# A fused attention, recurrence and convolution layer: first scales in the first input block, one matmul less at the start, last store from ACT, SBUF slots held back from the gates

## The chip, the cores and the metric

The kernel runs on one core of a Trainium2 chip. The metric is the device time of one execution in microseconds. A core has a matmul engine (PE), a vector engine (DVE), an activation engine (ACT), a general engine (POOL) and an engine that only issues transfers (SP). They run side by side, each in the order of its own instruction stream, and wait for one another by semaphores. Matmul results land in PSUM, which has 8 banks; everything else lies in SBUF.

## The reference

The kernel computes one layer of a sequence model for 512 positions and 1024 channels. Everything is float32.

```python
h = rmsnorm(x, norm_mix_g)
z = h @ w_in          # fq fk fv ff | hq hf hi hg | ca cb | gl   (gl: 3 gates of 1024)
ya = fox_attention(rmsnorm(fq), rmsnorm(fk), fv, log_sigmoid(ff))   # 6 heads of 64
yb = hgrn2_chunkwise(hq, -expm1(logf), hi, logf)                    # 4 heads, state 128 x 96
yb = rmsnorm(yb) * silu(hg)
yc = silu(layernorm(causal_dwconv(ca * sigmoid(cb))))               # 256 channels, 31 taps
gates = sigmoid(gl + gate_b)
x = x + (gates[0]*(ya @ wb_a) + gates[1]*(yb @ wb_b) + gates[2]*(yc @ wb_c)) @ w_out
h2 = rmsnorm(x, norm_ffn_g)
gate_in, value_in = split(h2 @ w_up)
x = x + (silu(causal_dwconv(gate_in)) * value_in) @ w_down
```

## The kernel before

Activations lie transposed: 8 blocks `x0` to `x7` of 128 channels by 512 positions. Every block is scaled with its column of `g1` (the first norm's gain) and split by `split_scaled` into a high and a low part, `x0h` and `x0l`. ACT makes the high part and DVE the low part. The weights come in units of 128 x 1024 (`wr_`, the raw load), which ACT copies to a high part (`wh_`) and DVE subtracts to a low part (`wl_`). A product is three matmuls, high x high, low x high and high x low, so that one weight unit takes 24 matmuls of 512 columns.

**The order is made before the program runs.** `body` does not issue instructions; it records them in program order with a `Plan`. `Plan.schedule` then plays the whole list through with assumed durations, engine by engine. Whenever an engine is free it takes the ready instruction with the lowest priority number, which is the program position plus a base such as `FIRST` or `EVAC`. The result is a fixed instruction stream for every engine. An instruction may only be taken if all tiles that it opens fit: `CAPS` gives the number of slots of each kind. The main ones are 75 SBUF slots `s` of 128 x 512, 8 PSUM banks `ps`, and at most 5 of these banks for the long products (`mm`) and 6 for everything else (`aux`). A DVE instruction that opens no new slot is never held back by this rule.

The stages, in program order: the product for `hi` (PSUM tiles `him`), whose first matmul needs `x0h` and the first weights `wr_hi`; `cb` and `ca`, the input of the convolution (`xca`); four HGRN heads, each with `hf` and `hq` products, transposes `khT`, chunk states `pst` and `st`, seven levels (for each a DVE difference `d`, two ACT exponentials, a DVE product `ql`, PE matmuls `pl`, and for the five short levels a masked copy `COPY_PREDICATED` of the result into `at`), then `pi`; the fox projections between the heads; six fox heads, each with scores `sp`, a DVE instruction that adds the mask `cB` to the scores and takes the minimum (`dd`, and the read of its accumulator `mn`), an exponential `pp`, transposes `ptp` and the result `po`; `conv()` with 60 taps, each one DVE instruction `cv<-xca,pr,cv`, 30 for each of two blocks; the `hg` products and their evacuation `xhg`; then the gates.

A gate is a unit `gl` of 24 matmuls; there are 24 of them (`gl00`, `gl01`, `gl02`, `gl10`, ...), recorded behind the heads and the convolution, so that in the stream they serve as filling between the heads' short matmuls. `evac` moves a gate from its PSUM bank to an SBUF slot, `gr`, with one DVE instruction, and frees the bank. The slot then stays taken until the branch products (`br`) use it. After that come `wo`, the feed-forward products `ug` and `uv`, and `dn`; each of the last 8 outputs is added to the residual on DVE and stored.

The lines of `schedule` that decide whether an instruction may be taken:

```python
need = {}
for n in op.uses:
    if n not in live:
        for k in self.kind[n]:
            need[k] = need.get(k, 0) + 1
if all(used[k] + c <= self.caps[k] for k, c in need.items()):
```

In the profile all instructions recorded through the plan stand on line L110, so that groups are told apart by the names of their tiles.

Of the kernel before, what the change touches and what calls it, by code (L numbers as in the profile page):

```python
# [10 lines left out]
F32 = mybir.dt.float32  # L11
# [36 lines left out]
for _name, _w in (("ident", 128), ("ones", 128), ("onesD", 32)):  # L48
# [1 line left out]
    _n += _w  # L50
NCST = _n
CAPS = {"s": 75, "bm": 2, "tiny": 24, "wraw": 3, "whi": 3, "wlo": 3, "ps": 8, "mm": 5, "aux": 6,
        "d": 2, "ed": 3, "cB": 4, "dd": 3, "pp": 3, "pT": 8}
NCB = NM * (NM + 1) // 2 * P
NLV = 2
NAHEAD = 6
NWARM = 5
FIRST, WPREP, STAT, EVAC, YOUT = -4000000, -3000000, -2000000, -1000000, -1000000


# [4 lines left out]
class Plan:  # L65
# [73 lines left out]
    def schedule(self):  # L139
        ops = self.ops  # L140
        last = {}
        for op in ops:
            op.left = len(op.deps)
            op.ready = 0.0
            for d in op.deps:
                d.users.append(op)
            for n in op.uses:
                last[n] = last.get(n, 0) + 1
        used = {k: 0 for k in self.caps}
        live = set()  # L150
        free = {e: 0.0 for e in ("tensor", "vector", "scalar", "gpsimd", "sync")}
        soon = {e: [] for e in free}
        now_ = {e: [] for e in free}
        releases = []
        for op in ops:
            if not op.left:
                heapq.heappush(soon[op.eng], (op.ready, op.seq, op))
        t, done, order = 0.0, 0, []
        while done < len(ops):
            while releases and releases[0][0] <= t:  # L160
                _, n = heapq.heappop(releases)
                for k in self.kind[n]:
                    used[k] -= 1
            for e in free:
                while soon[e] and soon[e][0][0] <= t:
                    op = heapq.heappop(soon[e])[2]
                    heapq.heappush(now_[e], (op.pri, op.seq, op))
            moved = False
            for e in free:
                if free[e] > t or not now_[e]:  # L170
                    continue
                put = []
                while now_[e]:
                    it = heapq.heappop(now_[e])
                    op = it[2]
                    need = {}
                    for n in op.uses:
                        if n not in live:
                            for k in self.kind[n]:
                                need[k] = need.get(k, 0) + 1  # L180
                    if all(used[k] + c <= self.caps[k] for k, c in need.items()):
                        for n in op.uses:
                            live.add(n)
                            last[n] -= 1
                        for k, c in need.items():
                            used[k] += c
                        op.start = t
                        op.end = t + op.dur
                        free[e] = op.end
                        for n in op.uses:  # L190
                            if not last[n]:
                                heapq.heappush(releases, (op.end + op.lat, n))
                        for u in op.users:
                            hop = 0.0 if (u.eng == e == "tensor") else op.lat
                            u.ready = max(u.ready, op.end + hop)
                            u.left -= 1
                            if not u.left:
                                heapq.heappush(soon[u.eng], (u.ready, u.seq, u))
                        order.append(op)
                        done += 1  # L200
                        moved = True
                        break
                    put.append(it)
                for it in put:
                    heapq.heappush(now_[e], it)
            if moved:
                continue
            nxt = [f for e, f in free.items() if f > t and now_[e]]
            nxt += [s[0][0] for s in soon.values() if s and s[0][0] > t]
            nxt += [max(s[0][0], free[e]) for e, s in soon.items() if s]  # L210
            if releases:
                nxt.append(releases[0][0])
            nxt = [x for x in nxt if x > t]
            if not nxt:
                raise RuntimeError("no instruction can start: " + str(
                    {e: [(o[2].seq, o[2].uses) for o in now_[e][:3]] for e in now_}) + str(used))
            t = min(nxt)
        self.length = max(op.end for op in ops)
        return order
# [57 lines left out]


@with_exitstack
def body(ctx: ExitStack, tc, xT, wct, wt3, wt1, wdn, par, cst, rst, msk, cmk, out):  # L280
    cpool = ctx.enter_context(tc.tile_pool(name="cpool", bufs=1))
    spool = ctx.enter_context(tc.tile_pool(name="spool", bufs=CAPS["s"]))
    wpool = ctx.enter_context(tc.tile_pool(name="wpool", bufs=3))
# [8 lines left out]
    def nm(name):  # L292
        cnt[0] += 1
        return f"{name}_{cnt[0]}"

    def slot(name, dt=F32, kind=None):
        return nc.tile(spool, [P, S], dt, "s", nm(name), ("s", kind) if kind else ("s",))
# [14 lines left out]
    def pc(name, i=0, n=1):  # L312
        o, _ = PCOLS[name]
        return pr[:, o + i:o + i + n]
# [57 lines left out]
    def split_scaled(src, g, name):  # L372
        hi = slot(name + "h", F32R)
        nc.scalar.activation(hi, src, AF.Copy, scale=g)
        lo = slot(name + "l", F32R)
        nc.vector.scalar_tensor_tensor(lo, src, g, hi.bitcast(F32), op0=ALU.mult, op1=ALU.subtract)
        return hi, lo

    def evac(ps, name, rb):
        with nc.at(EVAC):  # L380
            t = slot(name)
            nc.vector.tensor_tensor(t, ps, rb, op=ALU.mult)
        return t

# [62 lines left out]
    with nc.at(FIRST):  # L447
        nc.table("sigmoid_and_others")
        for _ in range(NWARM):
            nc.tensor.matmul(wps[:, :256], warm[:, :P], warm[:, :256], start=True, stop=True)  # L450
    cuts = ((0, 1), (1, 2), (2, 3), (3, 4), (4, 6), (6, 8))
    xg, w0, sums = [], [], []
    xs = [slot(f"x{kt}") for kt in range(KT)]

    def first_weights():
        k0, k1 = cuts[len(w0)]
        src = wt3[k0 // 2][:, (k0 % 2) * 384:(k0 % 2) * 384 + (k1 - k0) * 384]
        raw = nc.tile(bpool, [P, 2 * S], F32, "bm", nm("wr_hi"), ("bm",)) if len(w0) in (3, 4) else None
        w0.append(wunit(src, (k1 - k0) * 384, f"hi{len(w0)}", FIRST, raw))

    for kt in range(KT):
        with nc.at(FIRST):
            nc.sync.dma_start(xs[kt], xT[:, kt, :])
            if kt == 0:
                nc.sync.dma_start(pr[:, :KT], par[:, :KT])
            if kt == 4:
                nc.sync.dma_start(pr[:, KT:], par[:, KT:])
        if kt in (0, 1, 2, 3, 5):
            first_weights()
        with nc.at(FIRST):  # L470
            xg.append(split_scaled(xs[kt], pc("g1", kt), f"x{kt}"))
        with nc.at(STAT):
            q = slot(f"n1sq{kt}")
            added = nc.scalar.activation(q, xs[kt], AF.Square)
            if kt:
                nc.vector.tensor_tensor(sums[0], sums[0], q, op=ALU.add)
            else:
                sums.append(q)
# [448 lines left out]
    merged, gates, x1, xg2 = [], [], [], []  # L927

    def gate(n):
        gates.append([evac(gemm_c(15 + 3 * n + br, xg, f"gl{n}{br}"), f"gr{n}{br}", rb1) for br in range(3)])  # L930

    def merge(n):
        gts = gates[n]
# [59 lines left out]
    for n in range(KT):  # L993
        parts = ((0, S),) if n < KT - 1 else ((0, S // 2), (S // 2, S))
        ps = bank(f"dn{n}", "mm")
        ws = [wunit(wdn[n][:, k0 * P:min(NF, k0 + 8) * P], (min(NF, k0 + 8) - k0) * P, f"wd{n}{k0}")
              for k0 in range(0, NF, 8)]
        for w, k0 in zip(ws, range(0, NF, 8)):
            gemm_unit(ps, w, gT[k0:k0 + 8], k0 == 0, k0 + 8 >= NF)
        for c0, c1 in parts:  # L1000
            with nc.at(EVAC):
                nc.vector.tensor_tensor(x1[n][:, c0:c1], ps[:, c0:c1], x1[n][:, c0:c1], op=ALU.add)
            nc.sync.dma_start(out[n][:, c0:c1], x1[n][:, c0:c1])

    nc.issue(tc)

# [1 line left out]
def _layout(i):  # L1008
# [49 lines left out]
    for L in LEVELS:  # L1058
# [4 lines left out]
    c = np.ascontiguousarray  # L1063
    return {
        "xT": c(x.T.reshape(KT, P, S).transpose(1, 0, 2)), "wct": c(wct), "wt3": c(wt3), "wt1": c(wt1),
        "wdn": c(wdn), "par": c(par), "cst": c(cst), "rst": c(rst), "msk": c(msk), "cmk": c(cmk)}


_ORDER = ("xT", "wct", "wt3", "wt1", "wdn", "par", "cst", "rst", "msk", "cmk")


# [14 lines left out]
```

## Time and profile before

| | before |
|---|---|
| time, median of 3 runs (lowest, highest) | 804.49 us (804.33, 804.51) |
| the profiled execution's own time | 804.38 us |
| its span in the trace | 802.5 us |
| PE busy | 797.6 us, 99% of the span |
| DVE busy | 496.4 us, 62% |
| ACT busy | 336.6 us, 42% |
| POOL busy | 86.0 us, 11% |
| mean granted clock of PE | 0.999 of full speed |

The span is the stretch from the first to the last event of the trace; the profiled execution's time is 1.9 us longer. The busy share is an average over the stages.

### The profile page before, as it was taken

The numbers are of one execution on the slowest core, as the hardware profiler recorded it, in microseconds if no ns is written. First come the engines' busy times: TensorE is split into PE (matmuls) and PEld (weight loads), VectorE is DVE, ScalarE is ACT, GpSimd is POOL, SyncE is SP. The second block draws the span as 40 slices with busy tenths as digits, with TensorE's granted clock in tenths as the row PEclk, the third lists the DMA queues.
The fourth block names the chain that finished last, engine by engine and source line by source line (L and its number), as shares of the span: only waits on it lengthen the run. The fifth ranks groups of instructions, "written<-read, shape, count | busy, mean of one in ns | idle before, by whom it ended". The sixth has DMA issues, their size and how long they took to land.

```text
span 802.5 us, 10175 instructions
## 1 busy us (share of the span) xinstructions
PE 797.6 (99%) x3911; PEld 677.0 (84%) x3911; DVE 496.4 (62%) x804; ACT 336.6 (42%) x547; POOL 86.0 (11%) x78
## 2 busy tenths in 40 slices
PE   9999999999999999999999999999999999999998
PEld 8889999888888888888888888888888888888886
DVE  6588898988888878556655465555555455222221
ACT  7247556554656328433244254333333333111110
POOL 2000000100122000114422021111101111000000
PEclk9999999999999999999999999999999999999999
DMA  8522132422477222323422322322322332334320
GB/s 306 182 69 83 60 118 79 106 100 79 120 166 181 93 104 80 118 103 133 145 97 87 119 84 100 105 94 91 105 100 85 105 99 82 102 112 128 101 86 26
DMA packets 30880, 86.96 MB, mean 108 GB/s; under 512 B 3640, under 2 KB 7786, under 8 KB 30832
## 3 DMA queue, kind: packets, MB, share of 16 engines
q1 hardware_dynamic: 28240, 82.39, 30.3%
q0 software_dynamic: 2592, 3.93, 3.2%
q8 instruction: 30, 0.49, 0.3%
q14 instruction: 18, 0.15, 0.1%
HBM read 84.17 MB, written 2.14 MB: 108 GB/s over the span
## 4 chain that ended last, share of the span: by engine, by line
PE 99%; DVE 0%; DVEq 0%; issue 0%
PE gl L110 17%; PE ug L110 15%; PE uv L110 15%; PE dn L110 15%; PE br L110 5%; PE wo L110 5%; PE hf L110 3%; PE hq L110 3%; PE pl L110 3%; PE fvm L110 2%; PE him L110 2%; PE f0m L110 2%; PE f1m L110 2%; PE hg L110 2%; PE cb L110 1%; PE ca L110 1%
## 5 line engine op out<-in xcount | busy, mean ns | idle before, releaser
L110 DVE TENSOR_TENSOR wl_wd<-wr_wd,wh_wd 128x1024 fp32r<-128x1024 f32 (+1 forms) x24 | 27.3, 1136 | 65.9 <-ACT wh_wd L110 65.9
L110 ACT CAST wh_wd<-wr_wd 128x1024 fp32r<-128x1024 f32 (+1 forms) x24 | 23.6, 983 | 85.6 <-PE dn L110 81.8
L110 DVE TENSOR_TENSOR wl_ug<-wr_ug,wh_ug 128x1024 fp32r<-128x1024 f32 x22 | 27.0, 1225 | 49.6 <-ACT wh_ug L110 49.6
L110 POOL TENSOR_TENSOR fy<-fy,n2rB 128x512 f32<-128x512 f32 x22 | 28.9, 1317 | 207.8 <-ACT fy L110 207.8
L110 DVE SCALAR_TENSOR_TENSOR cv<-xca,pr,cv 128x511 f32<-128x511 f32 (+29 forms) x60 | 43.5, 729 | 0.3
L110 ACT CAST wh_uv<-wr_uv 128x1024 fp32r<-128x1024 f32 x22 | 23.2, 1054 | 44.4 <-PE ug L110 37.0
L110 ACT CAST wh_gl<-wr_gl 128x1024 fp32r<-128x1024 f32 x24 | 25.3, 1053 | 35.2 <-PE gl L110 21.4
L110 POOL DMA_DIRECT2D cB<-cdr x18 | 16.0, 1093 | 213.7 <-DMA cdr<-cT 122.8
L110 ACT CAST wh_ug<-wr_ug 128x1024 fp32r<-128x1024 f32 x22 | 23.2, 1055 | 31.1 <-PE uv L110 23.6
L110 POOL TENSOR_TENSOR gr<-gr,gr 128x512 f32<-128x512 f32 x14 | 21.6, 1546 | 113.9 <-DVE gr L110 113.2
L110 DVE SCALAR_TENSOR_TENSOR fy<-ug,pr,fy 128x511 f32<-128x511 f32 (+1 forms) x44 | 32.8, 747 | 1.0 <-ACT fy L110 0.3
L110 DVE TENSOR_TENSOR wl_gl<-wr_gl,wh_gl 128x1024 fp32r<-128x1024 f32 x24 | 31.5, 1311 | 2.3 <-ACT wh_gl L110 2.2
L110 DVE TENSOR_TENSOR gr<-gl,n1rB 128x512 f32<-128x512 f32 x24 | 16.6, 692 | 25.3 <-PE gl L110 25.3
L110 DVE TENSOR_TENSOR wl_uv<-wr_uv,wh_uv 128x1024 fp32r<-128x1024 f32 x22 | 27.0, 1225 | 8.5 <-ACT wh_uv L110 8.5
L110 DVE TENSOR_TENSOR ug<-ug,n2rB 128x512 f32<-128x512 f32 x22 | 15.1, 691 | 25.4 <-PE ug L110 25.3
L110 ACT ACTIVATE fy<-fy 128x512 f32<-128x512 f32 x22 | 13.9, 632 | 39.4 <-DVE fy L110 39.4
L110 PEld LDWEIGHTS pl<-ql,kl 128*128 128x128 f32 (+2 forms) x224 | 21.3, 161 | 2.2 <-issue 0.8
L110 DVE TENSOR_TENSOR x<-dn,x 128x512 f32<-128x512 f32 (+1 forms) x9 | 5.6, 631 | 27.3 <-PE dn L110 27.3
L110 PE MATMUL pl<-ql,kl 128*128 128x64 f32 (+2 forms) x224 | 21.3, 242 | 0.0
L110 DVE TENSOR_TENSOR gr<-gr,br 128x512 f32<-128x512 f32 x24 | 16.2, 682 | 5.5 <-PE br L110 5.4
L110 ACT ACTIVATE fy<-ug,pr 128x512 f32<-128x512 f32 x22 | 17.8, 812 | 1.9 <-DVE ug L110 1.9
L110 DVE TENSOR_TENSOR d<-bm 128x520 f32<-128x520 f32 (+5 forms) x24 | 18.1, 773 | 0.0
(1128 smaller groups left out, 2540.2 us busy)
## 6 DMA issues: line engine op xcount, KB each, us to landing
wr_gl<-wct SPq DMA_DIRECT2D x24, 512.0 KB, 3.2
wr_ug<-wct SPq DMA_DIRECT2D x22, 512.0 KB, 3.3
wr_uv<-wct SPq DMA_DIRECT2D x22, 512.0 KB, 3.3
wr_wd<-wdn SPq DMA_DIRECT2D x16, 512.0 KB, 3.5
x<-xT SPq DMA_DIRECT2D x16, 256.0 KB, 4.6
wr_wb<-wct SPq DMA_DIRECT2D x8, 512.0 KB, 3.2
wr_wo<-wct SPq DMA_DIRECT2D x8, 512.0 KB, 3.1
wr_wd<-wdn SPq DMA_DIRECT2D x8, 384.0 KB, 3.1
```

The lines of the kernel that those rows point to most:

```text
L110: op.fn = lambda: fn(*args, **kw)
```

## The change

It has four parts.

1. A new input `x0g` of 128 x 520 holds the first block of `x` and, behind it, the 8 columns of `g1`. One transfer brings both into a tile of the `bm` pool; the separate transfer of `pr[:, :8]` goes. DVE copies the 8 columns to `pr` for the later blocks; the first block's two scalings read them from the new tile. The raw tile of the fifth `hi` weight load moves from the `bm` pool to the `wraw` pool.
2. The warm-up at the start, 5 matmuls of 256 columns on zeros, becomes 4 of 256 and 1 of 128.
3. The last output block is stored in two halves; the second half's store is issued from ACT's queue instead of SP's.
4. The gates' slots get a kind of their own, `gr` (up to 24, as many as there are), and `schedule` takes an instruction that opens such a slot only if 3 more `s` slots would stay free behind it.

```diff
-        "d": 2, "ed": 3, "cB": 4, "dd": 3, "pp": 3, "pT": 8}
+        "d": 2, "ed": 3, "cB": 4, "gr": 24, "dd": 3, "pp": 3, "pT": 8}
-NWARM = 5
+NWARM = 4
@@ Plan.schedule
-                    if all(used[k] + c <= self.caps[k] for k, c in need.items()):
+
+                    spare = 3 if "gr" in need else 0
+                    if all(used[k] + c + (spare if k == "s" else 0) <= self.caps[k] for k, c in need.items()):
@@ body
-    def evac(ps, name, rb):
+    def evac(ps, name, rb, kind=None):
         with nc.at(EVAC):
-            t = slot(name)
+            t = slot(name, kind=kind)
             nc.vector.tensor_tensor(t, ps, rb, op=ALU.mult)
         return t
...
             nc.tensor.matmul(wps[:, :256], warm[:, :P], warm[:, :256], start=True, stop=True)
+        nc.tensor.matmul(wps[:, :P], warm[:, :P], warm[:, :P], start=True, stop=True)
-    xs = [slot(f"x{kt}") for kt in range(KT)]
+
+    x0 = nc.tile(bpool, [P, 2 * S], F32, "bm", nm("x0"), ("bm",))
+    xs = [x0[:, :S]] + [slot(f"x{kt}") for kt in range(1, KT)]
...
-        raw = nc.tile(bpool, [P, 2 * S], F32, "bm", nm("wr_hi"), ("bm",)) if len(w0) in (3, 4) else None
+        raw = nc.tile(bpool, [P, 2 * S], F32, "bm", nm("wr_hi"), ("bm",)) if len(w0) == 3 else None
...
-            nc.sync.dma_start(xs[kt], xT[:, kt, :])
             if kt == 0:
-                nc.sync.dma_start(pr[:, :KT], par[:, :KT])
+                nc.sync.dma_start(x0[:, :S + KT], x0g)
+                nc.vector.tensor_copy(pr[:, :KT], x0[:, S:S + KT])
+            else:
+                nc.sync.dma_start(xs[kt], xT[:, kt, :])
...
-            xg.append(split_scaled(xs[kt], pc("g1", kt), f"x{kt}"))
+            xg.append(split_scaled(xs[kt], pc("g1", kt) if kt else x0[:, S:S + 1], f"x{kt}"))
...
-        gates.append([evac(gemm_c(15 + 3 * n + br, xg, f"gl{n}{br}"), f"gr{n}{br}", rb1) for br in range(3)])
+        gates.append([evac(gemm_c(15 + 3 * n + br, xg, f"gl{n}{br}"), f"gr{n}{br}", rb1, "gr") for br in range(3)])
...
-            nc.sync.dma_start(out[n][:, c0:c1], x1[n][:, c0:c1])
+            (nc.sync if c1 - c0 == S or c0 == 0 else nc.scalar).dma_start(out[n][:, c0:c1], x1[n][:, c0:c1])
```

Since the order of every stream is made by `schedule`, the fourth part moves instructions on all engines from the first gate on. Three places follow, with the program's names and numbers of tiles (the second number of a name is only a serial number).

DVE's stream before, at the last `hg` evacuation (`xhg2`) and the mask-add of the first fox head's first scores (`dd_434`):

```order
L110 TENSOR_SCALAR nlk_380_467<-u_376_463,l1m_188 128x512
L110 ISA dd_434_521,mn_436_523<-sp_435_522,cB_427_514 128x128
L110 ISA mn_436_523 128x1
L110 TENSOR_TENSOR xhg2_689_776<-hg2_688_775,n1rB_78_158 128x512
L110 TENSOR_TENSOR bm_379_466<-bm_379_466,nlk_380_467 128x512
```

DVE's stream of the change from the same place on. `xhg2` stands 37 instructions before `dd_434`, and between the first and the last lines shown here stand 30 taps in all (5 of `cv0`, 25 of `cv1`, the last 20 of them in one row), three `wl_gl`, `qe` and `pr0`:

```order
L110 TENSOR_SCALAR nlk_380_467<-u_376_463,l1m_188 128x512
L110 TENSOR_TENSOR xhg2_689_776<-hg2_688_775,n1rB_78_158 128x512
L110 TENSOR_TENSOR bm_379_466<-bm_379_466,nlk_380_467 128x512
L110 TENSOR_TENSOR wl_gl02_711_798<-wr_gl02_709_796,wh_gl02_710_797 128x1024
...
L110 TENSOR_TENSOR wl_gl11_721_808<-wr_gl11_719_806,wh_gl11_720_807 128x1024
L110 SCALAR_TENSOR_TENSOR cv1_650_737<-xca1_102_182,pr_80,cv1_650_737 128x501
...
L110 SCALAR_TENSOR_TENSOR cv1_650_737<-xca1_102_182,pr_80,cv1_650_737 128x483
L110 SCALAR_TENSOR_TENSOR cv1_650_737<-xca1_102_182,pr_80,cv1_650_737 128x482
L110 ISA dd_434_521,mn_436_523<-sp_435_522,cB_427_514 128x128
L110 ISA mn_436_523 128x1
```

So `dd_434` moved from just before `xhg2` to 37 instructions behind it. The first gate's evacuation `gr00` stands 38 instructions behind `dd_434` in the change.

PE's stream before, at the transposes `khT_337` of HGRN head 2, which take the PSUM bank of `sp_435` and so wait for DVE's read of it:

```order
L110 MATMUL hg2_688_775<-x7h_47_127,wl_hg2_687_774 128x512
L110 MATMUL gl00_702_789<-x0h_14_94,wh_gl00_700_787 128x512
L110 MATMUL gl00_702_789<-x0l_15_95,wh_gl00_700_787 128x512
L110 MATMUL gl00_702_789<-x0h_14_94,wl_gl00_701_788 128x512
L110 MATMUL khT_337_424<-cs_78,kh_336_423 128x128 x3
L110 MATMUL gl00_702_789<-x1h_20_100,wh_gl00_700_787 128x512
```

PE's stream of the change at the same transposes:

```order
L110 MATMUL gl01_707_794<-x7l_48_128,wh_gl01_705_792 128x512
L110 MATMUL gl01_707_794<-x7h_47_127,wl_gl01_706_793 128x512
L110 MATMUL khT_337_424<-cs_78,kh_336_423 128x128 x3
L110 MATMUL pl_343_430<-ql_58_138,kl0_54_134 65x64 x4
L110 MATMUL pl_346_433<-ql_58_138,kl1_55_135 33x32 x8
L110 MATMUL pa_362_449<-pr0_361_448,cs_78 128x4
L110 MATMUL pl_349_436<-ql_58_138,kl0_54_134 128x64 x4
```

Before, three matmuls of the gate `gl00` stand between the last `hg` matmul and `khT_337`, and the rest of the gates fills in behind it. In the change all 48 matmuls of `gl00` and `gl01` stand ahead of it, and behind it no gate matmul follows until `gl02`, after 9 levels of `pl` (of heads 2 and 3), a second `khT`, six `pst`, seven `pi`, two `pa`, six `ptp` and four `sp`.

ACT's stream at the start, before:

```order
L137 ACT_TABLE_LOAD
L110 ACTIVATE n1sq0_16_96<-x0_3_83 128x512
L110 ACTIVATE x0h_14_94<-x0_3_83,pr_80 128x512
L110 CAST wh_hi0_12_92<-wr_hi0_11_91 128x384
L110 ACTIVATE x1h_20_100<-x1_4_84,pr_80 128x512
```

and in the change:

```order
L137 ACT_TABLE_LOAD
L110 ACTIVATE x0h_14_94<-x0_3_83 128x512
L110 CAST wh_hi0_12_92<-wr_hi0_11_91 128x384
L110 ACTIVATE n1sq0_16_96<-x0_3_83 128x512
L110 ACTIVATE x1h_20_100<-x1_4_84,pr_80 128x512
```

The square `n1sq0` moved behind the two instructions for which the first matmul waits.

## Rows read from the trace of the kernel before

**Rows 1.** The page: span, busy time of each engine, shares of the chain.

```profile
span 802.5 us, 10175 instructions
PE 797.6 (99%) x3911; PEld 677.0 (84%) x3911; DVE 496.4 (62%) x804; ACT 336.6 (42%) x547; POOL 86.0 (11%) x78
PE 99%; DVE 0%; DVEq 0%; issue 0%
```

**Rows 2.** Waits of PE: total us, times, longest us.

```profile
PE warm L110 <- DVE warm L110: 1.2, 1, 1.2
```

**Rows 3.** The chain of waits at head 2: start us, us, what.

```profile
162.27 16.35 PE hg L110 x72
...
179.31 0.33 PE khT L110 x3
...
186.14 0.64 PE pl L110 x16
...
188.59 0.84 PE pl L110 x8
...
191.10 0.84 PE pl L110 x8
```

**Rows 4.** The timeline of DVE at the end of `hg`: start us, us, instruction.

```profile
177.74 0.28 DVE L110 CUSTOM_DVE_ANT_0 dd<-sp,cB 128x128 f32<-128x128 f32 x1
...
178.66 0.69 DVE L110 TENSOR_TENSOR xhg<-hg,n1rB 128x512 f32<-128x512 f32 x1 [0.63 <-PE hg L110]
```

**Rows 5.** The timeline of DVE where four taps run in a row.

```profile
286.99 2.99 DVE L110 SCALAR_TENSOR_TENSOR cv<-xca,pr,cv 128x486 f32<-128x486 f32 x4
```

**Rows 6.** Groups of DVE by tile: count, busy us, mean ns, idle before.

```profile
L110 DVE SCALAR_TENSOR_TENSOR cv<-xca,pr,cv 128x511 f32<-128x511 f32 (+29 forms) x60 | 43.5, 729 | 0.3
L110 DVE TENSOR_TENSOR wl_gl<-wr_gl,wh_gl 128x1024 fp32r<-128x1024 f32 x24 | 31.5, 1311 | 2.3 <-ACT wh_gl L110 2.2
L110 DVE TENSOR_TENSOR d<-bm 128x520 f32<-128x520 f32 (+5 forms) x24 | 18.1, 773 | 0.0
L110 DVE CUSTOM_DVE_ANT_0 dd<-sp,cB 128x128 f32<-128x128 f32 (+3 forms) x24 | 11.2, 482 | 2.6 <-PE sp L110 1.4 <-DMA cB<-cdr 1.2
L110 DVE COPY_PREDICATED at<-mk,pl 128x256 f32<-128x256 uint8 x20 | 11.2, 560 | 3.9 <-PE pl L110 3.2 <-ACT kl L110 0.3
L110 DVE TENSOR_TENSOR ql<-ed,xq 128x256 f32<-128x256 f32 x24 | 10.0, 421 | 1.4 <-ACT ed L110 0.8 <-PE pl L110 0.6
```

**Rows 7.** Windows: length, busy PE PEld DVE ACT POOL, PEclk, DMA share, GB/s.

```profile
5.70:20.00 14.30, 14.27 (x80) 13.56 (x79) 12.60 (x21) 12.74 (x21) 0.66 (x2) 1.00 0.98 356
179.00:235.00 56.00, 56.00 (x380) 49.12 (x379) 47.79 (x115) 32.60 (x84) 6.60 (x8) 1.00 0.43 112
235.00:273.00 38.00, 38.00 (x223) 32.67 (x222) 32.47 (x84) 21.16 (x47) 5.72 (x7) 1.00 0.61 152
801.00:802.50 1.50, 0.00 (x0) 0.00 (x0) 0.00 (x0) 0.00 (x0) 0.00 (x0) 0.50 0.05 17
```

**Rows 8.** The timeline of the start.

```profile
1.18 0.42 SPq L110 DMA_DIRECT2D pr<-par  x1
1.19 4.63 PE L110 MATMUL warm<-warm 128*128 128x256 f32 x10 [1.19 <-DVE warm L110]
3.62 0.63 ACT L110 ACTIVATE n1sq<-x 128x512 f32<-128x512 f32 x1 [1.60 <-DMA x<-xT]
4.89 0.75 DVE L110 SCALAR_TENSOR_TENSOR x0l<-x,pr,x0h 128x512 fp32r<-128x512 f32 x1 [3.76 <-ACT x0h L110]
5.31 1.02 PE L110 MATMUL him<-wh_hi,x0h 128*128 128x384 f32 x3
```

**Rows 9.** The timeline of the end.

```profile
798.46 0.39 PE L110 MATMUL dn<-gT21h,wl_wd 128*128 128x512 f32 x1
798.89 0.76 DVE L110 TENSOR_TENSOR x<-dn,x 128x256 f32<-128x256 f32 x2 [13.36 <-PE dn L110]
799.34 0.82 SPq L110 DMA_DIRECT2D out<-x  x2
```

More of the change, by code (lines that the diff above doesn't have):

```diff
@@ L279, in body @@
 @with_exitstack
-def body(ctx: ExitStack, tc, xT, wct, wt3, wt1, wdn, par, cst, rst, msk, cmk, out):
+def body(ctx: ExitStack, tc, xT, wct, wt3, wt1, wdn, par, cst, rst, msk, cmk, x0g, out):
     cpool = ctx.enter_context(tc.tile_pool(name="cpool", bufs=1))
@@ L1065, in _layout @@
         "xT": c(x.T.reshape(KT, P, S).transpose(1, 0, 2)), "wct": c(wct), "wt3": c(wt3), "wt1": c(wt1),
-        "wdn": c(wdn), "par": c(par), "cst": c(cst), "rst": c(rst), "msk": c(msk), "cmk": c(cmk)}
-_ORDER = ("xT", "wct", "wt3", "wt1", "wdn", "par", "cst", "rst", "msk", "cmk")
+        "wdn": c(wdn), "par": c(par), "cst": c(cst), "rst": c(rst), "msk": c(msk), "cmk": c(cmk),
+        "x0g": c(np.concatenate([x.T[:P], par[:, :KT]], 1))}
+_ORDER = ("xT", "wct", "wt3", "wt1", "wdn", "par", "cst", "rst", "msk", "cmk", "x0g")
 def kernel(**inputs):
```

## Prediction

> **What bounds the kernel now.** I read the page first. PE is busy for 99% of the span, and the chain that ended last runs through PE alone [rows 1]. The waits of PE say the same: it waited once, 1.2 us for the memset of the warm-up [rows 2]. So no pause of PE is left to remove behind the start, and whatever makes PE stand adds to the time in full. Next I read who could make it stand. DVE is busy 62% on average, but in the stretch of the HGRN and fox heads it is 47.79 of 56 us and then 32.47 of 38, both 85%, while PE runs without a gap [rows 7]. There DVE's order decides when PE's short matmuls may start, and the gate matmuls that stand between them give it the time. A change of order in that stretch is the first thing to look at; the start and the end are small beside it.
>
> **Part 4, the slots held back, term A: the transposes of head 2.** In the order of before, DVE's mask-add `dd_434` stands just ahead of `xhg2`, and in the trace it began at 177.74, before `xhg2` at 178.66 [rows 4]. PE's `khT_337`, which waits for it, came at 179.31 without a wait [rows 3]. In the new order `dd_434` stands 37 instructions behind `xhg2`. `xhg2` cannot start before the last `hg` matmul, which is the same place in both orders. From there DVE has to do, before PE may begin `khT_337`:
> - 20 taps in a row. Four in a row took 2.99 us [rows 5], so 0.747 each, 14.9 in all.
> - 10 more taps at the mean of 0.729 [rows 6], 7.3.
> - three `wl_gl` at 1.31 [rows 6], 3.9.
> - `xhg2` at 0.69 [rows 4], `bm` and `qe`, of the same 512 columns, at the same; `pr0` about 0.15; `dd_434` with its read 0.3 [rows 4]. Together 2.5.
>
> That is 28.6 us. In the meantime PE has the 48 matmuls of `gl00` and `gl01`. The 72 `hg` matmuls of the same form took 16.35 [rows 3], so 0.227 each, 10.9 in all. DVE starts some 0.2 after PE does, because it reads what PE's last `hg` matmul wrote. PE then stands 28.6 + 0.2 - 10.9 = 17.9 us. The bounds are 16.9 (the three `wl_gl` and all taps at the quickest rows near) and 18.3. I take 17.8. Nothing covers it: PE takes its stream in order, so the work behind `khT_337` waits with it, also ACT's and DVE's on head 2.
>
> **Term B: the heads without filling.** Behind `khT_337` no gate matmul follows until `gl02`, and that one waits for a PSUM bank, which the evacuation `gr00` frees, 38 instructions behind `dd_434` on DVE. What DVE does until then: five `dd` at 0.482 and their reads, 2.8; eight `ql` at 0.421, 3.4; six `d` at 0.773, 4.6; five masked copies at 0.56, 2.8 [rows 6]; eight small ones, which I take as 2.1; `gr00` as `xhg`, 0.7 [rows 4]. The sum is 16.4. All 60 taps are done by then, so DVE has no filling either. PE's work in this stretch: seven levels at up to 0.84 and two at 0.64, 7.2; three transposes, 0.33 [rows 3]; 25 other short matmuls at about 0.17, 4.2; in all 11.7. If DVE never waits, PE stands 16.4 - 11.7 = 4.7. But each level goes from DVE to ACT, to DVE, to PE and back. In before, levels followed one another 2.5 us apart (188.59 and 191.10), of which 0.84 were the level and the rest gate matmuls [rows 3]. Nine levels at this pace take 22.5, with 1.7 for the `dd` ahead of them 24.2, so PE would stand 12.5. That pace had taps and gates in it, so it is the upper end. I take 8, a little under the middle.
>
> **Term C: the rest of the fox heads.** Summed in the same way with the durations of before, the instructions from `gr00` to the end of the last fox head are 56.6 us of DVE and 57.5 us of PE, with 49 fewer gate matmuls (11.1 us) among PE's than before; these run later, in a stretch where PE needs no filling. With sums so close DVE would have to be busy all the time for PE not to wait, and it has been at 85% [rows 7]. Where DVE waits for ACT or PE, PE may come to wait too: bounds 0 and 6. I take 2, because gate matmuls stand between the short ones again.
>
> **The clock.** A pause of PE costs more than itself. After the last matmul, at 798.46 [rows 9], the granted clock in the window of 801 to 802.5 is 0.50, the level of 1.2 GHz; in all windows with matmuls it is 1.00 [rows 7]. Term A makes such a pause in the middle of the program. What is done before the clock is back takes twice as long; the trace before has no such return in it. Bounds are 0 and 2.3, half of the 4.63 of the warm-up at the start [rows 8], as an estimate of a stretch in which PE comes out of rest. I take 1.5.
>
> **Parts 1 and 2, the start.** SP issues one transfer less ahead of `wr_hi`, 0.42; ACT does `n1sq`, 0.63, behind what the first matmul waits for; the warm-up is one pass of ten shorter, 4.63 / 10 = 0.46 [rows 8]. These lie beside one another: the first `him` (5.31) needs all three, so it comes some 0.4 to 0.6 earlier. The scalings of later blocks come earlier with it. But from 5.7 on the transfers are 0.98 busy [rows 7], so the input stream may take this back. Bounds -0.2 and -0.9 (0.42 + 0.46); I take -0.7. The new copy of 8 columns on DVE is some 0.1, in DVE's idle 3.76 before `x0l` [rows 8].
>
> **Part 3, the end.** Two stores take SP 0.82 to issue, the second waits for DVE's second half in any case (both halves 0.76 from 798.89) [rows 9]. At most 0.4 is gained, if the first issue held the second up. No store from ACT is in the trace; its price is bounded by the length of an ACT instruction, 0.63 [rows 8], above. I take -0.1. The Trainium skill, "DMA: Bandwidth & Descriptors", section "Issuing engines are not separate DMA queues", says that issuing from several engines only saves the sequencer's time of starting a transfer, since all share the DMA engines. By that rule the term would be up to -0.4; the sum goes by the row.
>
> **The sum,** against the profiled execution's own 804.38 (the span of 802.5 [rows 1] and 1.9 around it; the median of the runs, 804.49, is 0.1 above, so nothing is corrected for): 804.38 + 17.8 + 8 + 2 + 1.5 - 0.7 - 0.1 = 832.9. I say 833. All low ends together give 804.4 + 16.9 + 4.7 - 0.9 - 0.4 = 824.7, all high ends 804.4 + 18.3 + 12.5 + 6 + 2.3 - 0.2 + 0.6 = 843.9.
>
> **The rivals.**
> - *Term A alone.* The heads behind `khT_337` find their DVE work already done, or ACT's exponentials were run ahead while PE stood, and B and C vanish: 804.4 + 17.8 + 1.5 - 0.8 = 822.9. For it: ACT is only 42% busy [rows 1]. Against it: DVE's 16.4 us of term B are counted, and stand behind `dd_434` in its stream. Chance 0.06.
> - *The clock stays low through the heads.* If the scattered short matmuls behind the pause do not bring it back, the 11.7 us of PE work of term B take 23.4; with 3 of waiting PE loses 14.7 there in place of 8, and the first 10 us of term C cost 10 more or at least half of it. That gives 832.9 + 6.7 + 5 to 10 - 1.5, about 846. For it: the granted clock fell after matmuls ended [rows 7]. Against it: in before 1.00 stood through these heads, though with gates between. The Trainium skill, "TensorE: Matmul & The Clock Gate", section "HAM oscillation — how this bites in real kernels", tells of such a case: waits that throttle PE again before each bout of work, so that every bout begins at the low clock. By that rule the time would be that of this rival. Chance 0.11.
> - *The other side: not slower.* DVE gets to `dd_434` while PE is still at `gl00` and `gl01`, so that PE never stands, and only the start and the end act: 804.4 - 0.8 = 803.6, within 0.2% of before. For it: PE has shown no wait on DVE [rows 2]. Against it: the point from which it decides is 10.9 us for the 37 instructions; with 6.4 us for all that is no tap, the 30 taps would have to take 0.15 each, and they take 0.73 to 0.75 [rows 5, 6]. Chance 0.03, and 0.01 that the start gains more than 0.2%.
>
> **How the numbers follow.** The forecast has 0.79; its own range is 825 to 843. The rival with A alone ends at 822.9 and the low clock at 846, so 822 to 846 leaves out the not-slower case and the outer parts of both, under 2 in 10. What this kernel's measurement can tell from no change is about 0.2%, 1.6 us: slower by more than that 0.96, within it 0.03, faster 0.01.
>
> **What the changed profile would show.** Right: PE waits on DVE at `khT` once for about 17 to 18 us, from about 189; ahead of that DVE shows 20 taps in a row and, behind them, `dd`; further waits of PE at `pl`, some 5 to 12 us in sum; a granted clock under 1.00 just behind the pause; more gate matmuls behind the last `po`; the first `him` near 4.8. Wrong: no PE wait over 5 us there (then the order does not bind as I read it), or waits at `pl` beyond 13 us, or a slice of 0.50 over more than 10 us of work.

## The result and the profile after

The changed kernel takes 838.97 us (median of 4 runs, 837.07 to 840.03) against 804.45: a ratio of 1.0428, 95% interval 1.0414 to 1.0441. It is slower, inside the range of the prediction and 6 us above its number. The profiled execution took 838.8 with a span of 837.0.

The page of the changed kernel, in the lines that answer to [rows 1], with the granted clock in 40 slices:

```profile
span 837.0 us, 10167 instructions
PE 807.7 (96%) x3911; PEld 686.3 (82%) x3911; DVE 499.8 (60%) x805; ACT 336.2 (40%) x547; POOL 86.7 (10%) x78
PEclk9999999996599999999999999999999999999999
PE 95%; DVE 3%; DMA 1%; ACT 1%; issue 0%; DVEq 0%; SPq 0%; ACTq 0%
```

PE has the same 3911 matmul passes, is busy 10 us longer with them, and no longer fills the span. The clock falls in the tenth and eleventh slice, 188 to 230 us. The waits of PE, where [rows 2] had one line:

```profile
PE khT L110 <- DVE mn L110: 17.7, 1, 17.7
PE n1rT L110 <- DVE nry L110: 2.2, 1, 2.2
PE pl L110 <- DVE at L110: 1.4, 2, 0.9
...
PE po L110 <- DVE pl L110: 1.1, 1, 1.1
PE pst L110 <- DVE rl L110: 0.8, 1, 0.8
PE pl L110 <- DVE mn L110: 0.5, 1, 0.5
```

The first line is the wait that the prediction is built on. The second was not expected. The lines with `pl` and `pst` lie in the heads behind `khT` and sum to 2.7 us. The chain of waits from the end of `hg` (compare [rows 3]):

```profile
164.45 16.35 PE hg L110 x72
180.80 10.67 PE gl L110 x47
...
209.41 0.92 PE khT L110 x3
210.84 2.20 PE pl L110 x24
213.65 1.97 PE pl L110 x8
...
216.96 1.65 PE pl L110 x8
...
235.20 1.85 PE gl L110 x8
```

`hg` ends at 180.80 instead of 178.62, so 2.2 us are lost before it. `khT` comes at 209.41. A level of `pl` with 8 passes takes 1.65 where it follows other matmuls directly, and 1.97 where PE stood before it; it took 0.84 [rows 3]. Only at 235 does a gate matmul follow. DVE's timeline in the same stretch (compare [rows 4] and [rows 5]):

```profile
180.84 0.69 DVE L110 TENSOR_TENSOR xhg<-hg,n1rB 128x512 f32<-128x512 f32 x1 [0.47 <-PE hg L110]
...
183.25 3.95 DVE L110 SCALAR_TENSOR_TENSOR cv<-xca,pr,cv 128x486 f32<-128x486 f32 x6
...
188.32 2.65 DVE L110 SCALAR_TENSOR_TENSOR cv<-xca,pr,cv 128x483 f32<-128x483 f32 x4
...
192.61 1.23 DVE L110 TENSOR_TENSOR wl_gl<-wr_gl,wh_gl 128x1024 fp32r<-128x1024 f32 x1 [1.03 <-ACT wh_gl L110]
193.75 15.27 DVE L110 SCALAR_TENSOR_TENSOR cv<-xca,pr,cv 128x501 f32<-128x501 f32 x20
209.06 0.29 DVE L110 CUSTOM_DVE_ANT_0 dd<-sp,cB 128x128 f32<-128x128 f32 x1
```

The row of 20 taps stands ahead of `dd`, and PE starts `khT` when `dd` has been read. The windows of the stretch (columns as in [rows 7]):

```profile
195.00:200.00 5.00, 0.00 (x0) 0.00 (x0) 4.75 (x8) 0.00 (x0) 0.00 (x0) 0.50 0.26 97
215.00:220.00 5.00, 4.91 (x23) 4.53 (x24) 2.51 (x7) 2.44 (x6) 1.02 (x2) 0.50 0.53 99
230.00:235.00 5.00, 5.00 (x46) 4.84 (x46) 2.78 (x10) 2.58 (x9) 0.00 (x1) 0.77 0.37 79
235.00:240.00 5.00, 5.00 (x31) 4.30 (x30) 4.58 (x14) 4.68 (x15) 0.86 (x1) 1.00 0.34 59
```

The clock is at 0.50, the 1.2 GHz level, from the pause until shortly after 230, although PE is busy for most of 210 to 230. The 0.77 of the window from 230 to 235 puts the return to 1.00 near 232, some 3 us ahead of the first gate matmul.

**Where the 34.5 us of span came from,** by the times of the same PE instructions in both traces:

| stretch | before | after | lost |
|---|---|---|---|
| start to the end of `hg` | 178.62 | 180.80 | 2.2 |
| end of `hg` to `khT`, less 10.9 of gates | no wait | 28.6 | 17.7 |
| `khT` to `gl02`, less 11.7 of work | filled | 25.6 | 13.9 |
| `gl02` to the first `br` | the rest | the rest | 0.7 |
| first `br` to the end of the span | 483.6 | 483.6 | 0.0 |

The 11.7 is the prediction's estimate of PE's work there, so the third and the fourth row are as good as that estimate; their sum, 14.6, does not depend on it.

### The profile page after: what moved, and what is told of

The parts are those of the page before. It is cut to its first block, busy times and chain, and to the rows that moved or that the text cites. A ratio compares the mean times of both kernels' runs of the same rounds, so it can differ in the third digit from the quotient of the medians.

```text
span 837.0 us, 10167 instructions
## 1 busy us (share of the span) xinstructions
PE 807.7 (96%) x3911; PEld 686.3 (82%) x3911; DVE 499.8 (60%) x805; ACT 336.2 (40%) x547; POOL 86.7 (10%) x78
## 4 chain that ended last, share of the span: by engine, by line
PE 95%; DVE 3%; DMA 1%; ACT 1%; issue 0%; DVEq 0%; SPq 0%; ACTq 0%
PE gl L110 15%; PE ug L110 14%; PE uv L110 14%; PE dn L110 14%; PE wo L110 5%; PE br L110 5%; PE pl L110 3%; PE hf L110 3%; PE hq L110 3%; PE fvm L110 2%; PE him L110 2%; PE f0m L110 2%; PE f1m L110 2%; PE hg L110 2%; DVE cv L110 2%; PE ca L110 1%
## 5 line engine op out<-in xcount | busy, mean ns | idle before, releaser
L110 ACT CAST wh_uv<-wr_uv 128x1024 fp32r<-128x1024 f32 x22 | 23.2, 1054 | 44.4 <-PE ug L110 37.0
L110 ACT CAST wh_ug<-wr_ug 128x1024 fp32r<-128x1024 f32 x22 | 23.2, 1054 | 31.1 <-PE uv L110 23.6
L110 ACT ACTIVATE fy<-fy 128x512 f32<-128x512 f32 x22 | 13.9, 632 | 39.5 <-DVE fy L110 39.4
L110 PEld LDWEIGHTS pl<-ql,kl 128*128 128x128 f32 (+2 forms) x224 | 24.7, 188 | 3.3 <-DVE mn L110 0.9
L110 PE MATMUL pl<-ql,kl 128*128 128x64 f32 (+2 forms) x224 | 25.6, 272 | 1.2 <-DVE mn L110 0.5
L110 PE MATMUL khT<-cs,kh 128*128 128x128 f32 x12 | 3.4, 351 | 17.7 <-DVE mn L110 17.7
L110 ACT ACTIVATE fy<-ug,pr 128x512 f32<-128x512 f32 x22 | 17.8, 811 | 1.9 <-DVE ug L110 1.9
```

Source lines behind the costliest of these rows:

```text
L110: op.fn = lambda: fn(*args, **kw)
```

## The experiments

The order that `schedule` makes is plain to read, and it gave the next question before any run. With the new start and 0 spare slots `schedule` ends with "no instruction can start", while before with the rule of part 4 has `dd_434` where it always was. So part 4 may not be what moved `dd_434`. Two facts of the order point to the start. First, on DVE the last step of the first norm's reciprocal root (`nry2`) and the low part of the second `ca` weights (`wl_ca1`) have changed places. Before:

```order
L110 TENSOR_TENSOR nra_73_153<-nra_73_153,nv_66_146 128x4
L110 SCALAR_TENSOR_TENSOR nry2_74_154<-nra_73_153,nry1_72_152 128x4
L110 TENSOR_TENSOR wl_ca1_100_180<-wr_ca1_98_178,wh_ca1_99_179 128x1024
```

and in the change:

```order
L110 TENSOR_TENSOR nra_73_153<-nra_73_153,nv_66_146 128x4
L110 TENSOR_TENSOR wl_ca1_100_180<-wr_ca1_98_178,wh_ca1_99_179 128x1024
L110 SCALAR_TENSOR_TENSOR nry2_74_154<-nra_73_153,nry1_72_152 128x4
```

Second, `schedule` refuses `dd_434` for lack of an `s` slot: in the changed order ACT's `kh` of head 3 opens the 75th slot before `dd_434` is ready, the next one that comes free goes to `qe` of head 3, and the one behind it comes free when the last tap has read its input. In before `dd_434` takes that slot and `kh` waits. This is theory S: the swap at the start shifts everything behind it, `kh` wins the last slot, and the taps have to finish first. Theory R is the prediction's: the rule of part 4 moves `dd_434`.

**The rule alone.** The kernel before with part 4.

```diff
...
-                    if all(used[k] + c <= self.caps[k] for k, c in need.items()):
+                    spare = 3 if "gr" in need else 0
+                    if all(used[k] + c + (spare if k == "s" else 0) <= self.caps[k] for k, c in need.items()):
...
```

> The kernel before with part 4 alone (the gates' own kind and the 3 spare slots). Theory R, the one of the prediction: the rule moves the first mask-add dd_434 behind the taps. It would then show PE waiting about 17.7 us at khT, and about 830 to 836 us. Theory S, formed from the trace of the change: the rule does not move it; in the changed order the 75 slots were full when dd_434 was ready, because head 3's kh had taken the last one, and that came from the start. In this kernel's order dd_434 stands ahead of xhg2 as before and 3 gate matmuls ahead of khT, so S expects no wait at khT and 804.5, within 1.5.

Measured: 809.56, ratio 1.0064 (1.0047 to 1.0081). No wait at `khT`, so theory R falls. But the rule is not free either, which S had not expected: 5.1 us. The waits of PE in this run and its windows (columns as in [rows 7]):

```profile
PE pl L110 <- DVE at L110: 1.0, 1, 1.0
PE pa L110 <- DVE at L110: 0.8, 1, 0.8
PE pl L110 <- ACT kl L110: 0.3, 1, 0.3
```

```profile
195.00:200.00 5.00, 3.05 (x20) 2.83 (x21) 4.95 (x12) 2.92 (x10) 0.00 (x0) 0.85 0.30 105
200.00:205.00 5.00, 5.00 (x29) 5.00 (x28) 2.99 (x8) 2.46 (x7) 1.38 (x2) 0.50 0.52 125
205.00:210.00 5.00, 5.00 (x46) 4.44 (x46) 3.71 (x10) 3.52 (x10) 1.19 (x2) 0.97 0.64 128
```

With `gr00` and `gr01` held back, `gl02` comes at 208.65, 14 us behind the last matmul of `gl01` at 194.30, with only short ones between. 2.1 us of the loss are waits. By the three windows (0.85, 0.50, 0.97) the clock was at 0.50 for 6.8 us, and at half the rate that is 3.4 us of work lost, an estimate. Together they come to 5.5, and the two traces differ by 5.6 (spans of 808.1 and 802.5). This is term B of the prediction in small.

**The root ahead of the weights.** The change with one dependence, which undoes the swap.

```diff
...
+            with nc.after(*(rs[2:3] if name == "ca1" else ())):
-            nc.vector.tensor_tensor(lo[:, :n], raw[:, :n], hi[:, :n].bitcast(F32), op=ALU.subtract)
+                nc.vector.tensor_tensor(lo[:, :n], raw[:, :n], hi[:, :n].bitcast(F32), op=ALU.subtract)
...
```

(`rs[2]` is the instruction that writes `nry2`.)

> The change with one dependence more: DVE's low part of the second ca weights (wl_ca1) comes only after the last step of the first norm's reciprocal root (nry2), as it stood before. Theory S: the swap of these two instructions costs the 2.2 us wait of PE at n1rT, and its delay in the planner lets kh take the last slot, so one dependence takes away n1rT's 2.2, khT's 17.7 and the slow heads behind it: 804.2, between 803 and 806. Theory R (the 3 spare slots move dd_434): only the 2.2 go, 836.8.

Measured: 809.61, ratio 1.0064 (1.0049 to 1.0079). The waits at `n1rT` and `khT` are both gone, and besides the warm-up's the same three as in the run above are left. That is 29.4 us of the 34.5 with one dependence. What is left is the price of the rule that the run above showed, which the number given for S did not contain.

**A slot for the mask-add.** The change with the swap, where `kh` and `qe` must leave one slot free.

```diff
...
-                    spare = 3 if "gr" in need else 0
+                    spare = 3 if "gr" in need else 1 if "kh" in need else 0
-        qe = slot("qe")
+        qe = slot("qe", kind="kh")
-        kh = slot("kh")
+        kh = slot("kh", kind="kh")
```

> The change with one spare slot also held back from kh and qe, so that the first mask-add gets one; the swap at the start stays. In its order dd_434 stands 4 instructions behind xhg2, with 17 gate matmuls (3.9 us) ahead of khT. If the missing slot is what delays dd_434, PE does not wait at khT for more than 1 us, the 2.2 at n1rT stay, and the time is 806.4, up to 810 if the later gate evacuations leave waits in the heads. If the slot is not the cause, 839.

Measured: 816.81, ratio 1.0154 (1.0137 to 1.0171). The longest waits of PE:

```profile
PE n1rT L110 <- DVE nry L110: 2.2, 1, 2.2
...
PE pl L110 <- DVE at L110: 0.8, 1, 0.8
```

No wait at `khT`, the 2.2 at `n1rT` stay: the missing slot is what delays `dd_434`. The time is above the 810 expected, again by the rule; a later run takes it away.

**Filling the pause.** The change with 72 matmuls ahead of `khT` that add zeros (a tile of 128 x 128, filled once at the start) to the finished sum of `gl01`; no other instruction moves.

```diff
...
             for op in order:
                 op.fn()
+                if op is last:
+                    for k in range(72):
+                        self.fill(k == 71)
...
```

> The change with 72 matmuls that add zeros to gl01's bank, 16.3 us of PE work, put into the pause ahead of khT; every other instruction stands where it stood. Clock theory: the heads behind the pause took 25.6 us because the granted clock was 0.50 there; with the pause filled it stays 1.00, khT comes at the same time, and khT to gl02 takes 16.4 (DVE's sum) to 20, so 829.5 to 833.5. Rival: DVE's and ACT's chain sets the pace of these heads whatever the clock, 25.6 stays and the time is 839.

Measured: 835.88, ratio 1.0396 (1.0370 to 1.0422). `khT` waits 0.9 and comes at 209.22. The rows of PE behind it and two windows:

```profile
209.22 0.55 PE L110 MATMUL khT<-cs,kh 128*128 128x128 f32 x3 [0.95 <-DVE mn L110]
210.29 1.46 PE L110 MATMUL pl<-ql,kl 128*65 128x64 f32 x24 [0.52 <-DVE mn L110]
...
212.38 1.97 PE L110 MATMUL pl<-ql,kl 128*128 128x64 f32 x8
...
234.14 0.40 PE L110 MATMUL gl<-x0h,wh_gl 128*128 128x512 f32 x1
```

```profile
209.00:215.00 6.00, 5.14 (x41) 4.69 (x42) 4.39 (x12) 2.59 (x7) 0.86 (x1) 0.69 0.26 76
215.00:220.00 5.00, 4.92 (x24) 4.53 (x24) 3.04 (x7) 2.40 (x6) 0.86 (x1) 0.50 0.58 92
```

`khT` to `gl02` takes 24.9 us where the change took 25.6. The clock was up when `khT` began and fell in the first window, near 211 by its 0.69, behind the waits of 0.95 and 0.52 us. It then stayed at 0.50 while PE was busy 4.92 of 5 us. So the long pause is not what keeps the clock low in the heads. The number given for the clock theory is missed, and so is the rival's 839: the median lies 3.1 us under the change's, of which the heads make 0.7. This leaves open whether the low clock or DVE and ACT pace these heads.

**Filling the heads.** The same, with 3 more of these matmuls ahead of each of 10 groups of short ones between `khT` and `gl02`, and in a second kernel 6.

```diff
...
             for op in order:
+                if op in heads:
+                    for k in range(3):
+                        self.fill(op is heads[-1] and k == 2)
                 op.fn()
...
```

> The change with the pause filled as before (72 matmuls adding zeros to gl01's bank) and 3 more such matmuls ahead of each of 10 groups of short matmuls (pl, pst, pi) between khT and gl02: 30 more, 6.8 us of PE work that nobody needs. Without them khT to gl02 took 24.9 us, at a granted clock of 0.50, of which 2.9 were waits. Clock theory, second form (the clock falls because these heads hold nothing but short matmuls): the added work keeps the clock at 1.00, and 11.7 + 6.8 of work and 1 to 4 of waits make 19.5 to 22.5, so that more work takes less time: 830.5 to 833.5. Rival (DVE's and ACT's chain paces the heads): the added work goes into the waits or on top, 24.9 to 29, so 836 to 840.

> The same with 6 instead of 3 ahead of each group: 60 matmuls, 13.6 us. Clock theory: 25.3 of work at 1.00 and waits under 1.5, so 25.3 to 26.8 from khT to gl02, 836.3 to 837.8, and the granted clock 1.00 there. Rival: with the clock at 0.50 the work alone is 23.4 and 13.6 at the best, 37 us, so 848.

Measured: 834.84, ratio 1.0381 (1.0367 to 1.0395), and 840.13, ratio 1.0446 (1.0432 to 1.0461). First the kernel with 3, its windows and its first gate matmul behind the heads:

```profile
209.00:215.00 6.00, 6.00 (x54) 5.06 (x55) 4.26 (x10) 2.73 (x8) 0.86 (x1) 1.00 0.26 76
215.00:220.00 5.00, 4.80 (x35) 4.08 (x34) 3.71 (x9) 3.21 (x10) 0.86 (x1) 1.00 0.55 92
220.00:225.00 5.00, 4.01 (x23) 3.33 (x23) 3.68 (x10) 2.96 (x13) 0.00 (x0) 0.86 0.16 39
225.00:230.00 5.00, 5.00 (x31) 4.21 (x29) 1.61 (x7) 1.44 (x5) 0.86 (x1) 0.79 0.40 82
```

```profile
208.97 0.55 PE L110 MATMUL khT<-cs,kh 128*128 128x128 f32 x3 [0.95 <-DVE mn L110]
...
232.17 0.40 PE L110 MATMUL gl<-x0h,wh_gl 128*128 128x512 f32 x1
```

With 6.8 us of work added, `khT` to `gl02` takes 23.2 us, 1.7 less than without. That lies between the two expectations, 0.7 above the clock theory's upper end and 1.7 under the rival's lower one. With 13.6 added it takes 27.8, and in all windows of that kernel from 209 to 240 the clock is 1.00; one of them stands below its two rows:

```profile
209.85 0.55 PE L110 MATMUL khT<-cs,kh 128*128 128x128 f32 x3 [0.95 <-DVE mn L110]
...
237.66 0.40 PE L110 MATMUL gl<-x0h,wh_gl 128*128 128x512 f32 x1
```

```profile
215.00:220.00 5.00, 5.00 (x36) 4.51 (x35) 2.49 (x5) 1.98 (x5) 1.16 (x2) 1.00 0.59 109
```

27.8 is far from the 37 that the rival gave and 1 above the clock theory's upper end; the time of 840.13 is 2.3 above that end. The difference in the stretch, 1.7, is larger than the one in the times of the two kernels, 1.0, whose ranges overlap (833.77 to 839.0 and 833.87 to 836.06), and they come from two sessions, so the 1.7 rests on one trace of each. That the clock was low for less time holds for all executions: its mean is 0.986 to 0.993 in the four with the pause filled and 0.998 to 1.000 in the four with 3 more ahead of each group.

What this shows is that PE at 0.50 fills most of the stretch in the change: it waits 2.7 of the 25.6 us. How long the heads would take at 1.00 with nothing added was not measured, and DVE's and ACT's chain may then be the bound. The added matmuls are wide and also cover waits between the short ones; which of the two holds the clock was not separated.

**Without the rule.** The change with 0 spare slots and the root ahead of the weights.

```diff
...
-                    spare = 3 if "gr" in need else 0
+                    spare = 0 if "gr" in need else 0
...
```

> The change without the rule (0 spare slots instead of 3) and with the reciprocal root ahead of wl_ca1: what is left are the first block with its scales, the shorter warm-up and the store from ACT. The gates are evacuated as early as before. The start was 0.45 earlier at the end of hg in the run with the root put ahead, the end was the same within 0.05. So 804.0, 0.4 under before, if the rule alone made the 5.2 us of that run; 809 if something else of the new order did.

Measured: 803.52 (11 runs, 803.37 to 804.01) against 804.32, ratio 0.9991 (0.9982 to 1.0000). PE waits only at the warm-up. The end of `hg` is at 178.07, 0.55 earlier than before. So the rule makes 6.1 us of the 809.6 with the root ahead.

**The warm-up and the store alone,** in the kernel before.

```diff
-NWARM = 5
+NWARM = 4
+        nc.tensor.matmul(wps[:, :P], warm[:, :P], warm[:, :P], start=True, stop=True)
-            nc.sync.dma_start(out[n][:, c0:c1], x1[n][:, c0:c1])
+            (nc.sync if c1 - c0 == S or c0 == 0 else nc.scalar).dma_start(out[n][:, c0:c1], x1[n][:, c0:c1])
```

> The kernel before with parts 2 and 3 alone: the shorter warm-up and the last half-store from ACT's queue. PE's first him waits for ACT's copies, not for the warm-up, so nothing at the start; the store's end moved by 0.04 in the change. 804.4, within 0.3.

Measured: 804.23, ratio 1.0000 (0.9991 to 1.0008). Parts 2 and 3 do nothing that can be measured.

**The swap and the rule in the kernel before.** The first block, the warm-up and the store stay as they were.

```diff
...
+        if name == "ca1":
+            rs[2].deps.add(op)
...
```

(`op` is the subtraction of `wl_ca1`; part 4 as in the first experiment.)

> The kernel before with part 4 and one dependence that puts the last step of the reciprocal root (nry2) behind wl_ca1, as it stands in the change; the first block, the warm-up and the store are those of before. In its order dd_434 stands 37 instructions behind xhg2 and 48 gate matmuls ahead of khT, as in the change. Theory S (the swap of two instructions at the start, through the planner's slots, is the cause): the whole loss comes with it, 804.3 + 2.5 at n1rT + 17.7 at khT + 14 in the heads + 0.7 = 839, within 2. Rival (the new first block is needed for it): under 815.

Measured: 839.20, ratio 1.0441 (1.0425 to 1.0456): the whole loss of the change, without its first block. The waits of PE and DVE's rows:

```profile
PE khT L110 <- DVE mn L110: 17.7, 1, 17.7
PE n1rT L110 <- DVE nry L110: 2.2, 1, 2.2
```

```profile
195.43 15.28 DVE L110 SCALAR_TENSOR_TENSOR cv<-xca,pr,cv 128x501 f32<-128x501 f32 x20
210.75 0.29 DVE L110 CUSTOM_DVE_ANT_0 dd<-sp,cB 128x128 f32<-128x128 f32 x1
```

**The slot without the rule.** The third experiment with 0 in place of 3.

```diff
-                    spare = 3 if "gr" in need else 1 if "kh" in need else 0
+                    spare = 0 if "gr" in need else 1 if "kh" in need else 0
```

> The change with one spare slot held back from kh and qe, but without the rule for the gates; the swap at the start stays. Here dd_434 stands 4 instructions behind xhg2 and the gates are evacuated early, so only the swap's own wait at n1rT is left: 803.5 + 2.5 = 806, up to 808 if the order leaves waits. If the 12.4 us of the run with both came from the late khT (17 gate matmuls ahead of it) and not from the rule, 814.

Measured: 807.72 (806.5 to 809.49), ratio 1.0052 (1.0036 to 1.0069). Besides the warm-up's, `n1rT` is PE's only wait, 2.2 us. So the rule made 9.1 us of the third experiment's time, and the swap, with the slot held back, costs 4.2 against 803.52, more than its wait. The profiled execution, at 806.5, is 3.0 above it; the last section has a possible reason for the slower ones, which were not traced.

**One spare slot instead of 3,** with the root ahead.

```diff
...
-                    spare = 3 if "gr" in need else 0
+                    spare = 1 if "gr" in need else 0
...
```

> The change with the root put ahead and 1 spare slot instead of 3. gr00 stands at DVE's row 297; with no spare it stands at 280, with 3 at 317. With 3 the rule cost 6.1 us (809.6 against 803.5), because gl02 could not start for lack of a bank and the heads ran without gates at a clock of 0.50. If the cost goes with the row of gr00, about 806.4; the gates' rows between the pl of head 2 and khT of head 3 are still there, so the clock should fall less long, 804.5 to 807.

Measured: 806.99, ratio 1.0040 (1.0025 to 1.0055), 3.5 above no spare slot, where 3 cost 6.1.

## Why the prediction came out as it did

**Term A held, mechanism and size.** PE waits once at `khT` for DVE's read, 17.7 us where 17.8 were said, behind the 20 taps in a row that take 15.27 us. The wait for `wh_gl`, 1.03, was not in it, and the 20 taps took 0.4 more than said; it came out because rows that overlap in the pipeline made up for both: the other 10 taps took 6.6 instead of 7.3, and DVE went on 1.14 us behind the start of each `wl_gl` instead of 1.31.

**Its cause was put in the wrong place.** The prediction headed it "Part 4, the slots held back", and the text on the change says that the fourth part moves the instructions. The number did not suffer, since it was read off the finished order. The runs show that the rule alone leaves `dd_434` where it was and costs 5.1; that undoing the swap of `nry2` and `wl_ca1` takes 29.4 of the 34.5 us away; and that the swap with the rule brings the whole loss to the kernel before. The swap comes with part 1: the order that `schedule` makes for parts 1 and 4 alone has the swap and `dd_434` where the change has them, and the one for parts 2, 3 and 4 has neither. The norm's sums (`n1ms`) start at 24.78 in the change and at 24.13 before. Without the rule this order does not exist, since `schedule` finds none. An order that is made from one list is not split into parts by where the diff's lines stand.

**Term B failed in size and in mechanism: 13.9 instead of 8, and above its upper bound of 12.5.** The step had PE stand and wait for DVE. PE waits 2.7 us in this stretch. The other 11 come from the step's price of PE's work, 11.7 at the full clock with a term of its own of 1.5 for the pause: the short matmuls without gates among them ran at 0.50, 1.65 for a level instead of 0.84, and their work then took most of the 25.6 us. Filling the pause shortened the heads by 0.7 only; filling the heads brought the clock back. The prediction's own sign of being wrong, a slice of 0.50 over more than 10 us of work, did show: the clock was low for some 23 us of work. Its sign of being right, 5 to 12 us of waits at `pl`, did not: there are 1.9.

**The rival with the low clock had that much right.** It named term B as 14.7, with 3 of waiting and the rest from work at 0.50; B was 13.9, with 2.7 of waiting. Its other half, a low clock in the first part of term C, did not come: from 235 on the clock is 1.00. The Trainium skill, "TensorE: Matmul & The Clock Gate", section "HAM oscillation — how this bites in real kernels", has the throttle follow from waits between bouts of work. The trace of the kernel whose pause was filled agrees in part: the clock fell behind waits of 0.95 and 0.52 us, but then stayed at 0.50 with PE busy 4.92 of 5 us.

**Term C** was 0.7 where 2 were said.

**The start failed in sign.** The step said -0.7, bounds -0.2 and -0.9. The first `him` does come 0.26 earlier (5.05), and the last product of `hi` 0.27. The swap then costs 2.2 at `n1rT`, since `wl_ca1` waits for ACT and the four columns of `nry2` stand behind it:

```profile
30.17 1.23 DVE L110 TENSOR_TENSOR wl_ca<-wr_ca,wh_ca 128x1024 fp32r<-128x1024 f32 x1 [1.44 <-ACT wh_ca L110]
31.31 0.15 DVE L110 SCALAR_TENSOR_TENSOR nry<-nra,nry 128x4 f32<-128x4 f32 x1
```

The prediction followed the order only to the first `him` and from the end of `hg` on, and not between. With the swap undone the start gives 0.55 at the end of `hg`.

**The end** was -0.04 where -0.1 was said: between the last matmul and the end of the span lie 3.6 us in both kernels. SP and ACT issue their stores one behind the other, because DVE's halves come one behind the other:

```profile
833.90 0.34 SPq L110 DMA_DIRECT2D out<-x  x1
834.23 0.37 ACTq L110 DMA_DIRECT2D out<-x  x1
```

**The rival on the other side** failed at its point of decision, the price of a tap: 20 took 15.27 us, 0.76 each, and the other 10 took 0.66 each, against the 0.15 that it needed. The three edits that the change could gain by do so only without the rule and the swap: 803.52, at most 0.2% under before by its interval.

**The total was in part luck.** Against the sum of 832.9, term A was 0.1 under, B and the clock together 4.4 over, C 1.3 under, the start 2.9 over, the end 0.1 over. The range held because the largest term was right and because the bounds of the others were wide enough for a mechanism that B did not have.

## What to carry to other kernels

Where a list scheduler makes the order, compare its whole output for every engine, and look at each place where two instructions have changed sides around a wait: here two DVE instructions at 30 us decided who got the last buffer at 180. Filling matmuls may do more than cover the waits of short ones. In the change, and in the runs with the rule alone and with the filled pause, the heads without filling ran at 0.50 for nearly 7 us or more; before, and with 6 filling matmuls ahead of each group, they ran at 1.00. So a stretch of short matmuls that has lost its filling is to be priced at the low level as well. A rule that keeps buffers from early results can take away the work that fills later stalls, so price what it stops.

## What the runs showed of the hardware that was not expected

More matmuls took less time, in one trace of each: 30 wide ones (6.8 us) added to a stretch of short ones made it 23.2 instead of 24.9 us, with the granted clock at 1.00 and 0.79 to 0.86 in place of 0.50. How much wide work among short ones is needed was not found out; with 13.6 us it stayed at 1.00. And it also came back without any: in the change it rose near 232, when PE had run short matmuls alone since 209.

One and the same pause may or may not cost the clock. PE waits 2.24 us at `n1rT` in the change and in the kernel with the swap and the rule, and the matmuls behind the wait are the same. The window behind it, first of the change, then of the other:

```profile
32.00:34.00 2.00, 2.00 (x11) 1.64 (x10) 0.11 (x1) 1.50 (x4) 0.00 (x0) 1.00 0.67 198
```

```profile
32.00:34.00 2.00, 2.00 (x6) 1.62 (x5) 0.15 (x1) 1.54 (x4) 0.00 (x0) 0.50 0.68 193
```

In the second case `hg` ends 1.7 us later than in the first (182.48 against 180.80), though the wait ends at the same point (31.52 and 31.56). The seven traces with this wait split: behind it the clock is at 0.50 in three and at 1.00 in four. The loss is of the size of the spread that the kernel with the swap and without the rule shows: its executions at 806.5 and 806.73 have a mean clock of 1.000, those at 808.71 and 809.49 of 0.998 and 0.999. That this wait is where they lost it is not shown.
